# Keeping all seven output-weight phases as split halves in DRAM

## The chip, the cores and the metric

The kernel runs on one core of a Trainium2 chip. The metric is the time of one execution on the device, in microseconds (us); the median of several runs is compared. TensorE (PE) does the matrix products, VectorE (DVE), ScalarE (ACT) and GpSimd (POOL) the rest, and SyncE (SP) issues the transfers between DRAM and on-chip memory.

## What is computed

Two layers on a sequence of 2048 rows of 1024 features in float32: first a gated MLP with mixing in groups of 128 rows, then attention with 16 heads of 64 over bands of nine chunks of 64 rows, with keys and values from the stream between the two, and a final norm. The change lies in the last step of the attention layer, the product with `w_out`:

```
q, z = jnp.split(h @ w_qz, 2, axis=-1)
...
o = lax.map(one_chunk, (jnp.arange(n_chunks), q))     # scores + bias, softmax, times v
o = jnp.moveaxis(o, 0, 1).reshape(bsz, s, B_WIDTH)
return (o * jax.nn.silu(z)) @ w_out                   # 2048 x 1024 times 1024 x 1024
...
x = x + chunk_attention_mixer(...)
return rms_norm(x, final_norm_g)
```

## The kernel before

A float32 product is done as three TensorE passes on pairs of reduced-precision numbers: each operand is split into a high part (a cast on ScalarE, `split_in` L228) and a low part (operand minus high part, a subtraction on VectorE, L229), and `mm3` (L111 to L113) adds high times high, high times low and low times high.

The attention stage works on four tiles of 512 rows, t = 0 to 3, and in each on eight head pairs p. For a pair the kernel projects the next pair's q, k and gate (`pj`, weights `raw_b` split to `wh_b` and `wl_b`), makes scores (`s`, L1469), softmax (`pr`, `nm`, `sl`), transposes (`tp`, L1504), copies to `pt` on ScalarE and VectorE (L1508, L1509) and multiplies with V (`pv`, L1529).

The output projection `bo` of a tile uses Strassen's scheme for a 2 by 2 block product: seven phases instead of eight block products, done in the order 1, 7, 2, 6, 5, 4, 3. Each phase has one weight block, loaded in two pieces q = 0, 1 of 512 KB, and two output column blocks jp = 0, 1 of twelve matmuls each. Phases 1, 2 and 3 use plain quarters of `w_out` (`o_raw`): whenever one is used, its raw piece is loaded (`raw_bo`) and split. Phases 4 to 7 use sums of quarters. These are made and split once, early, and their high and low parts are kept in the DRAM tensors `ows`, so that each use loads two pieces of 512 KB and splits nothing.

The projection of tile t (names `bo` with the tile's number; the function is `o_right`) runs in portions between the pairs of tile t+1: that of the third tile, t = 2, runs beside the last tile's attention. For the last tile `last_right` gets the weights (`whbo`, `wlbo`, and `wbo` for phases 5 and 3) and `last_all` does the products, the first of them beside the last pair's softmax. Split weights live in eight rotating slots of tag `T` (`w_tile`), which the projections' `wh_b` and `wl_b` share; a slot takes a new tile when the last reader of the old one is done. In the last tile, phase 2 uses slots of tag `raw`, phase 5 a slot of `V`, phase 3 one of `PT`.

The order of instructions on each engine comes from a scheduler that works on the program before it runs; `on_beat` ties an instruction to the pace of the pair loop. Every transfer is issued by SP, in order, and at most eight are in flight: one waits for the eighth before it.

Of the kernel before, what the change touches and what calls it, by code (L numbers as in the profile page):

```python
# [9 lines left out]
F32 = mybir.dt.float32  # L10
# [12 lines left out]
NT = S // T  # L23
# [10 lines left out]
def trunk_kernel(  # L34
# [19 lines left out]
    nc = tc.nc  # L54
# [10 lines left out]
    }  # L65
    ows = {
        (ph, q): dram.tile([P, 2, 1024], F32, name=f"ows{ph}_{q}")
        for ph in range(4, 8) for q in range(2)
    }
    khd = [  # L70
        [dram.tile([2, P, T], F32, name=f"khd{t}_{p}") for p in range(NPAIR)]
# [49 lines left out]
    sub, add = ALU.subtract, ALU.add  # L121
    tv, tg = nc.vector.tensor_tensor, nc.gpsimd.tensor_tensor
# [70 lines left out]
    def on_beat(ins):  # L193
        if beat:
            tc.add_manual_dep(
                ins.ins, beat[-1],
                mybir.DependencyInfo(mybir.DependencyClass.NoSync, mybir.DependencyReason.DATA),
                reason="order",
            )
        return ins  # L200
# [16 lines left out]
    def w_tile(name):  # L217
        return sh.tile([P, 1024], F32R, tag="T", name=name, bufs=8)
# [3 lines left out]
    def raw_w(t, name):  # L222
        if t:
            return raws[0].tile([P, 1024], F32, tag="wr", name=name, bufs=2)
        return sh.tile([P, 1024], F32, tag="raw", name=name, bufs=4)

    def split_in(raw, wh, wl):
        hi = nc.scalar.copy(wh[:], raw[:])  # L228
        tv(wl[:], raw[:], wh[:].bitcast(F32), op=sub)  # L229
        return hi  # L230
# [26 lines left out]
    o_raw = {1: (0, 0), 2: (1, 0), 3: (1, 1)}  # L257

    def o_right(t):
        def right(ph):  # L260
            if (t, ph) in o_early:
                return o_early.pop((t, ph))
            out = []
            for q in range(2):
                name = f"bo{t}_{ph}_{q}"
                w = [w_tile(f"w{i}_{name}") for i in "hl"]
                if ph in o_raw:
                    raw = raw_w(1, f"raw_{name}")
                    nc.sync.dma_start(raw[:], wb_out[o_raw[ph]][q])
                    hi = split_in(raw, *w)  # L270
                    if (ph, q) == (1, 1):
                        on_beat(hi)
                else:
                    for i in range(2):
                        nc.sync.dma_start(w[i][:].bitcast(F32), ows[ph, q][:, i, :])
                out.append(w)
            return out
        return right
# [105 lines left out]
    with ExitStack() as actx:  # L384
# [21 lines left out]
        sub, add, mul = ALU.subtract, ALU.add, ALU.mult  # L406
# [650 lines left out]
        tv, tg = nc.vector.tensor_tensor, nc.gpsimd.tensor_tensor  # L1057
# [303 lines left out]
    with ExitStack() as bctx:  # L1361
# [16 lines left out]
        def half_tile(tag, name, bufs, dtype=F32):  # L1378
            return sb.tile([P, 512], dtype, tag=tag, name=name, bufs=bufs)
# [157 lines left out]
        def drain_all():  # L1537
            while drains:
                drains.pop(0)()
# [28 lines left out]
        def square_all(every=False):  # L1568
            if every:
                squares.extend(young)  # L1570
                young.clear()
            while squares:
                on_beat(squares.pop(0)())
            squares.extend(young)
            young.clear()

        owed_out = []

        def send(dst, src):
            if la:  # L1580
                owed_out.append((dst, src))
            else:
                nc.sync.dma_start(dst, src)

        def send_all():
            while owed_out:
                on_beat(nc.sync.dma_start(*owed_out.pop(0)))
# [96 lines left out]
        def last_right(ph, q):  # L1684
            name = f"bo_{ph}_{q}"
            if ph == 5:
                v = sb.tile([P, 8, 256], F32R, tag="V", name=f"w{name}", bufs=2)
                w = [v[:, i * 4 : i * 4 + 4, :].rearrange("p a b -> p (a b)") for i in range(2)]
            elif ph == 3:
                if q == 0:  # L1690
                    lw["pt"] = sb.tile([P, 5376], F32R, tag="PT", name=f"w{name}", bufs=1)
                w = [lw["pt"][:, (2 * q + i) * 1024 : (2 * q + i + 1) * 1024] for i in range(2)]
            elif ph == 2:
                w = [
                    sh.tile([P, 1024], F32R, tag="raw", name=f"w{i}{name}", bufs=4)[:]
                    for i in "hl"
                ]
            else:
                w = [w_tile(f"w{i}{name}")[:] for i in "hl"]
            if ph in o_raw:  # L1700
                raw = raw_w(NT - 1, f"raw_{name}")
                nc.sync.dma_start(raw[:], wb_out[o_raw[ph]][q])
                nc.scalar.copy(w[0], raw[:])
                tv(w[1], raw[:], w[0].bitcast(F32), op=sub)
            else:
                for i in range(2):
                    nc.sync.dma_start(w[i].bitcast(F32), ows[ph, q][:, i, :])
            lw[ph, q] = w

        lviews = {}  # L1710
# [13 lines left out]
        def last_all():  # L1724
# [6 lines left out]
            for q in range(2):  # L1731
                last_right(7, q)
# [164 lines left out]
        def take(gen, n):  # L1897
            for _ in range(n):
                if next(gen, gen) is gen:
                    return  # L1900

        def run(gen):
            for _ in gen:
                pass
# [16 lines left out]
        def ahead(t, p):  # L1921

            if t > 1 and p == 0:
                next(outs[t - 1])
            if p + 1 < NPAIR:
                yield from project(t, p + 1)
                values(t, p + 1)
                for q in GATES[t][p]:
                    yield from gate(t, q)
                if (t, p) == (1, 4):  # L1930
                    next(outs[0])
                yield from some(outs[t - 1], SHARE[t][p])
            elif t + 1 < NT:
                yield from some(outs[t - 1], SHARE[t][p])
                yield from border(t)
                yield from project(t + 1, 0)
                values(t + 1, 0)
                yield from gate(t + 1, 0)
            else:
                yield from some(outs[t - 1], SHARE[t][p] - 6)  # L1940
                last_first()
                yield from some(outs[t - 1], 6)
                yield from some(outs[t], 13)

        def steps_of(t, p):
            n = 24
            if p + 1 < NPAIR:
                n = 16 + 8 * len(GATES[t][p])
            elif t + 1 == NT:
                n = 13  # L1950
            return n + SHARE[t][p]
# [11 lines left out]
        for t in range(NT):  # L1963
            for p in range(NPAIR):
                gen = ahead(t, p) if t + p else first
                total = steps_of(t, p) - (0 if t + p else 8)
                per = 11 if p + 1 == NPAIR and t + 1 < NT else 16
                todo = []
                if t + 1 == NT and p + 1 == NPAIR:
                    o_early[t - 1, 3] = o_right(t - 1)(3)  # L1970
                    todo = last_open()
                if t == 1 and p < 4:
                    todo = o_sums(p, lambda n: half_tile("C", n, 4), lambda n: half_tile(
                        "S", n, 4, F32R
                    ))
                if (t, p) == (0, 3):
                    nc.sync.dma_start(gf[:], fin_g.partition_broadcast(P))
                done = 0
                for u in range(8):
                    if u < 6:  # L1980
                        score(t, p, u + 2)
                    elif p + 1 < NPAIR or t + 1 < NT:
                        score(t + (p + 1) // NPAIR, (p + 1) % NPAIR, u - 6)
                    upto = total * (2 * u + 1) // per
                    take(gen, upto - done)
                    done = max(done, upto)
                    if u == 4:
                        value(t, p, 0)
                    elif u == 0 and before:
                        value(*before, 1)  # L1990
                    flip(t, p, u)
                    drain_all()
                    send_all()
                    square_all()
                    if u and finals:
                        finals.pop(0)()
                    if todo:
                        todo.pop(0)()
                    upto = total * (2 * u + 2) // per
                    take(gen, upto - done)  # L2000
                    done = max(done, upto)
                if t + 1 < NT or p + 1 < NPAIR:
                    run(gen)
                before = t, p
# [61 lines left out]
```

## Time and profile before

| | |
|---|---|
| median of three runs | 2646.81 us (2646.17 to 2648.61) |
| the profiled execution | 2649.25 us, of which the span of work is 2647.5 |
| granted TensorE clock | 0.997 of full speed |
| TensorE busy | 2607.3 us, 98% of the span |
| VectorE, ScalarE, GpSimd busy | 71%, 49%, 34% |
| moved by DMA | 718.74 MB, on average 271 GB/s |

The profile is of one execution. Times in it count from the start of the span. A group row has line, engine, operation, output and inputs by the program's names, count, then busy us and the mean ns of one, then the engine's idle time before these instructions and what ended it. A row of waits has the waiting engine and line, the releaser, and the waiting time in us, the number of waits and the longest. Rows of DMAs end with the median us from issue to landing. Attention on the last tile takes the stretch from about 2300 to 2605 us; from there only the last projection and the final norm are left.

### The profile page before, as it was taken

Reading aid. Unit: us, or ns where it says so; the run is one execution under the profiler, and the core shown is the slowest. Engines: PE = TensorE matmul, PEld = TensorE weight load, DVE = VectorE, ACT = ScalarE, POOL = GpSimd, SP = SyncE. Lnnn points to the kernel's source line nnn. Section 1 sums busy time; section 2 is a strip of 40 time slices with the busy share of each in tenths; the row PEclk is TensorE's granted clock in tenths of the full one; section 3 lists DMA queues with packets and bytes.
Section 4 is the critical chain, followed back from the end, with each engine's and each line's share of the span. In section 5 each row is a group of like instructions: output and inputs, shape, how many; then the busy total and the mean of one; then the engine's idle time right before and its main releaser. Section 6 shows DMA issues by size and latency. Waiting matters only on the chain. (4 is left out here: it accounts for less than half of the span.)

```text
span 2647.5 us, 38028 instructions
## 1 busy us (share of the span) xinstructions
PE 2607.3 (98%) x12976; PEld 2179.8 (82%) x12976; DVE 1889.1 (71%) x2946; ACT 1303.1 (49%) x2303; POOL 893.7 (34%) x874
## 2 busy tenths in 40 slices
PE   8999999999999999999999999999999999999997
PEld 7888888888888888888878778888888888888886
DVE  6655676766767668757777767778778777877677
ACT  5422243443433434343356456666666655666564
POOL 4611335143152322203234434344332232332245
PEclk9999999999999999999999999999999999999999
DMA  7898998989988868967776587778787666875666
GB/s 291 313 347 331 345 367 321 315 324 340 335 318 294 311 235 328 328 201 270 282 266 209 194 284 229 233 240 264 251 269 258 224 208 220 256 229 159 195 227 249
DMA packets 273857, 718.74 MB, mean 271 GB/s; under 512 B 28800, under 2 KB 68736, under 8 KB 273664
## 3 DMA queue, kind: packets, MB, share of 16 engines
q1 hardware_dynamic: 273664, 716.31, 78.2%
q8 instruction: 104, 1.70, 0.3%
q14 instruction: 89, 0.73, 0.1%
HBM read 531.12 MB, written 174.59 MB: 267 GB/s over the span
## 5 line engine op out<-in xcount | busy, mean ns | idle before, releaser
L111 PE MATMUL P<-T,S 128*128 128x512 f32 x1248 | 495.7, 397 | 0.0
L113 PE MATMUL P<-T,S 128*128 128x512 f32 x1248 | 488.1, 391 | 0.1
L112 PE MATMUL P<-T,S 128*128 128x512 f32 x1248 | 487.8, 391 | 0.2 <-DVE T L444 0.2
L1488 POOL TENSOR_SCALAR pr<-pr,sl 128x640 f32<-128x640 f32 (+4 forms) x256 | 206.9, 808 | 553.9 <-DVE sl L1487 467.4
L111 PE MATMUL pj<-hh_b,wh_b 128*128 128x512 f32 x768 | 319.9, 417 | 0.7 <-ACT wh_b L228 0.7
L113 PE MATMUL pj<-hh_b,wl_b 128*128 128x512 f32 x768 | 304.2, 396 | 0.8 <-DVE wl_b L229 0.7
L112 PE MATMUL pj<-hl_b,wh_b 128*128 128x512 f32 x768 | 302.9, 394 | 0.1
L1484 ACT ACTIVATE pr<-pr,nm 128x640 f32<-128x640 f32 (+4 forms) x256 | 195.5, 764 | 186.2 <-DVE nm L1477 184.8
L113 PEld LDWEIGHTS P<-T,S 128*128 128x128 f32 x1248 | 234.6, 188 | 50.9 <-DVE S L444 0.4
L112 PEld LDWEIGHTS P<-T,S 128*128 128x128 f32 x1248 | 235.3, 189 | 45.3 <-DVE T L444 0.6
L111 PEld LDWEIGHTS P<-T,S 128*128 128x128 f32 x1248 | 235.2, 188 | 44.8 <-DVE x L577 0.4
L1509 DVE TENSOR_TENSOR pt<-tp,pt 128x640 fp32r<-128x640 f32 (+4 forms) x256 | 188.5, 736 | 43.8 <-ACT pt L1508 41.2
L1477 DVE CUSTOM_DVE_ANT_0 pr<-s,bias 128x640 f32<-128x640 f32 (+4 forms) x256 | 188.1, 735 | 32.5 <-PE s L1469 27.2
L1508 ACT CAST pt<-tp 128x640 fp32r<-128x640 f32 (+4 forms) x256 | 159.0, 621 | 54.1 <-PE tp L1504 49.7
L1504 PE MATMUL tp<-ident,pr 128*128 128x128 f32 x1120 | 166.5, 274 | 9.6 <-DVE pt L1509 7.8
L113 PEld LDWEIGHTS pj<-hh_b,wl_b 128*128 128x128 f32 x768 | 144.4, 188 | 35.7 <-DVE wl_b L229 2.9
L1504 PEld LDWEIGHTS tp<-ident,pr 128*128 128x128 f32 x1120 | 130.6, 140 | 44.3 <-issue 14.6
L111 PEld LDWEIGHTS pj<-hh_b,wh_b 128*128 128x128 f32 x768 | 145.3, 189 | 18.8 <-ACT wh_b L228 2.4
L1529 PEld LDWEIGHTS pv<-pt,V 128*128 128x128 f32 x896 | 143.0, 188 | 20.2 <-DVE pt L1509 3.2
L112 PEld LDWEIGHTS pj<-hl_b,wh_b 128*128 128x128 f32 x768 | 145.3, 189 | 16.9 <-DVE hl_b L186 0.5
L1529 PE MATMUL pv<-pt,V 128*128 128x256 f32 (+3 forms) x896 | 153.9, 319 | 1.9 <-ACT pt L1508 1.0
L229 DVE TENSOR_TENSOR wl_b<-raw_b,wh_b 128x1024 fp32r<-128x1024 f32 x96 | 120.2, 1253 | 28.2 <-ACT wh_b L228 27.0
(302 smaller groups left out, 5732.7 us busy)
## 6 DMA issues: line engine op xcount, KB each, us to landing
S<-hsd SPq DMA_DIRECT2D x288, 512.0 KB, 5.5
rw<-in_w_a SPq DMA_DIRECT2D x108, 512.0 KB, 6.5
A<-ytd SPq DMA_DIRECT2D x72, 512.0 KB, 5.8
raw_b<-wk SPq DMA_DIRECT2D x72, 512.0 KB, 4.3
hsd<-S SPq DMA_DIRECT2D x56, 512.0 KB, 4.7
V<-vhd SPq DMA_DIRECT2D x56, 512.0 KB, 5.6
bias<-reld SPq DMA_DIRECT2D x64, 320.0 KB, 3.9
va<-vd SPq DMA_DIRECT2D x32, 512.0 KB, 6.0
```

Source lines behind the costliest of these rows:

```text
L111: first = mm(ps, lh, rh, start=first, stop=False)
L112: mm(ps, lh, rl, start=False, stop=False)
L113: mm(ps, ll, rh, start=False, stop=last)
L229: tv(wl[:], raw[:], wh[:].bitcast(F32), op=sub)
L1477: nc.vector.tensor_tensor_reduce(out=pr[:, c0:].rearrange("p (a b) -> p a b", a=nseg), in0=ps[:, :nseg, :w], in1=bias[:, c0:].rearrange("p ...
L1484: nc.scalar.activation(pr[:, c0:], pr[:, c0:], AF.Exp, scale=-1.0, bias=nm[:], accum_out=sl[:])
L1488: nc.gpsimd.tensor_scalar(pr[:, c0:], pr[:, c0:], sl[:], 1.0, op0=ALU.mult, op1=ALU.mult)
L1504: ins = tpose(tp[:, b, :], pr[:, b * P : (b + 1) * P], ident[:])
L1508: nc.scalar.copy(oh, tp[:, b0:5, :].rearrange("p a b -> p (a b)"))
L1509: nc.vector.tensor_tensor(pt[:, 2560 + o + b0 * P : 2560 + o + 640], tp[:, b0:5, :].rearrange("p a b -> p (a b)"), oh.bitcast(F32), op=ALU ...
L1529: mm(po[:, q0 * P : q1 * P], vtl[t, p][:, i, hs], rhs, start=(i == blocks[0] and j == 0), stop=(i == 7 and j == 1),)
```

## The change

`ows` gets entries for phases 1 to 3. The splits are kept where they are made: those of phase 3 in the second tile's projection, those of phases 1 and 2 in the third tile's. Each gives four stores of 512 KB (two pieces, high and low), twelve in all, queued in `halves_out` and issued from ScalarE, one per step of the pair loop. The third tile's phase 3 and the last tile's phases 1, 2 and 3 load halves and split nothing: eight casts and eight subtractions are gone, and eight raw loads are sixteen loads of halves.

```diff
     ows = {
         (ph, q): dram.tile([P, 2, 1024], F32, name=f"ows{ph}_{q}")
-        for ph in range(4, 8) for q in range(2)
+        for ph in range(1, 8) for q in range(2)
     }
...
                 w = [w_tile(f"w{i}_{name}") for i in "hl"]
-                if ph in o_raw:
+                if ph in o_raw and (t, ph) != (2, 3):
                     raw = raw_w(1, f"raw_{name}")
                     nc.sync.dma_start(raw[:], wb_out[o_raw[ph]][q])
                     hi = split_in(raw, *w)
                     if (ph, q) == (1, 1):
                         on_beat(hi)
+                    if (t, ph) in ((2, 1), (2, 2), (1, 3)):
+                        halves_out.extend(
+                            (ows[ph, q][:, i, :], w[i][:].bitcast(F32)) for i in range(2)
+                        )
                 else:
                     for i in range(2):
                         nc.sync.dma_start(w[i][:].bitcast(F32), ows[ph, q][:, i, :])
...
         owed_out = []
+        halves_out = []
...
                 w = [w_tile(f"w{i}{name}")[:] for i in "hl"]
-            if ph in o_raw:
-                raw = raw_w(NT - 1, f"raw_{name}")
-                nc.sync.dma_start(raw[:], wb_out[o_raw[ph]][q])
-                nc.scalar.copy(w[0], raw[:])
-                tv(w[1], raw[:], w[0].bitcast(F32), op=sub)
-            else:
-                for i in range(2):
-                    nc.sync.dma_start(w[i].bitcast(F32), ows[ph, q][:, i, :])
+            for i in range(2):
+                nc.sync.dma_start(w[i].bitcast(F32), ows[ph, q][:, i, :])
             lw[ph, q] = w
...
                     send_all()
+                    if halves_out:
+                        on_beat(nc.scalar.dma_start(*halves_out.pop(0)))
                     square_all()
```

The scheduler's order changes around these places. Names in the rows that follow have lost the tile's number; `wh_bo_1_0` is the high part of phase 1, piece 0. The line numbers after the change are 4 to 5 higher.

ScalarE beside the third tile's phase 1, in the last tile's second pair. Before:

```order
L228 CAST wh_bo_1_1_22775<-raw_bo_1_1_22777 128x1024
L1508 CAST pt_1_22661<-tp_1_3_22816 128x640
L1484 ACTIVATE pr_2_1_22801,sl_2_1_22803<-pr_2_1_22801,nm_2_1_22802 128x640
L1847 COPY ou_1_0_22814<-bo_1_0_22781 128x512
L337 CAST Sho_7_0_22839<-A_s_22450 128x512
L1484 ACTIVATE pr_2_2_22848,sl_2_2_22850<-pr_2_2_22848,nm_2_2_22849 128x640
L228 CAST wh_b_2_1_22856<-raw_b_2_1_22855 128x1024
L1484 ACTIVATE pr_2_3_22909,sl_2_3_22911<-pr_2_3_22909,nm_2_3_22910 128x640
```

After, the same stretch:

```order
L228 CAST wh_bo_1_1_22785<-raw_bo_1_1_22787 128x1024
L1994 DMA ows_0_102<-wh_bo_1_0_22779 128x1024
L1512 CAST pt_1_22671<-tp_1_3_22826 128x640
L1488 ACTIVATE pr_2_1_22811,sl_2_1_22813<-pr_2_1_22811,nm_2_1_22812 128x640
L1846 COPY ou_1_0_22824<-bo_1_0_22791 128x512
L341 CAST Sho_7_0_22850<-A_s_22460 128x512
L1488 ACTIVATE pr_2_2_22859,sl_2_2_22861<-pr_2_2_22859,nm_2_2_22860 128x640
L228 CAST wh_b_2_1_22867<-raw_b_2_1_22866 128x1024
L1994 DMA ows_0_102<-wl_bo_1_0_22780 128x1024
L1488 ACTIVATE pr_2_3_22921,sl_2_3_22923<-pr_2_3_22921,nm_2_3_22922 128x640
```

Two stores have come in; the cast `wh_b_2_1` writes the slot that the first of them reads, and the subtraction `wl_b_2_1` on VectorE the slot of the second.

TensorE at the same place, from the first use of `wh_b_2_1`. Before:

```order
L111 MATMUL pj_2_1_22861<-hh_b,wh_b_2_1_22856 128x512
L112 MATMUL pj_2_1_22861<-hl_b,wh_b_2_1_22856 128x512
L1529 MATMUL pv_1_22865<-pt_1_22661,V_0_22347 128x512 x4
L113 MATMUL pj_2_1_22861<-hh_b,wl_b_2_1_22857 128x512
L1529 MATMUL pv_1_22865<-pt_1_22661,V_0_22347 128x128 x2
```

After:

```order
L111 MATMUL pj_2_1_22872<-hh_b,wh_b_2_1_22867 128x512
L112 MATMUL pj_2_1_22872<-hl_b,wh_b_2_1_22867 128x512
L1533 MATMUL pv_1_22876<-pt_1_22671,V_0_22357 128x512 x4
L1533 MATMUL pv_1_22876<-pt_1_22671,V_0_22357 128x128 x2
L1533 MATMUL pv_1_22876<-pt_1_22671,V_0_22357 128x256 x2
L1533 MATMUL pv_1_22876<-pt_1_22671,V_0_22357 128x384 x4
L1533 MATMUL pv_1_22876<-pt_1_22671,V_0_22357 128x256 x2
L1533 MATMUL pv_1_22876<-pt_1_22671,V_0_22357 128x128 x2
L1473 MATMUL s_3_0_22949<-K_1_1_22694,Ql_1_1_22570 128x320 x2
L113 MATMUL pj_2_1_22872<-hh_b,wl_b_2_1_22868 128x512
```

The first use of `wl_b_2_1` (L113) has moved behind twelve `pv` and two score matmuls.

SP before the last tile's first phases. Before:

```order
L1633 DMA A_hh<-ogd_145 128x512 x2
L1583 DMA x2d_1_155<-ou_7_0_23202 128x512
L1702 DMA raw_bo_0_25247<-in_wb_out 128x1024
L1702 DMA raw_bo_1_25253<-in_wb_out 128x1024
L1821 DMA y_1_25218<-x2d_1_155 128x1024
L1707 DMA wbo_0_25456<-ows_0_104 128x1024
L1587 DMA x2d_3_157<-ou_7_1_23567 128x512
L1707 DMA wbo_0_25456<-ows_0_104 128x1024
L1702 DMA raw_bo_0_25358<-in_wb_out 128x1024
```

After:

```order
L1638 DMA A_hh<-ogd_151 128x512 x2
L1592 DMA x2d_3_163<-ou_7_1_23581 128x512
L1820 DMA y_1_25232<-x2d_1_161 128x1024
L1706 DMA whbo_0_25259<-ows_0_102 128x1024
L1706 DMA wlbo_0_25260<-ows_0_102 128x1024
L1706 DMA whbo_1_25263<-ows_1_103 128x1024
L1706 DMA wlbo_1_25264<-ows_1_103 128x1024
L1592 DMA out<-y_1_25232 128x512 x2
```

Phase 1's two raw loads have become four loads of halves, and they stand behind the store `x2d_3` and the load `y_1`. The very end of TensorE's queue is mixed anew too: before, the last phase's column block `bo_0` is done before `bo_1` starts; now the two alternate, and `bo_0` ends five matmuls before `bo_1`.

## The prediction

> **What bounds the kernel now.** I read the page's busy times first.
>
> ```profile
> span 2647.5 us, 38028 instructions
> PE 2607.3 (98%) x12976; PEld 2179.8 (82%) x12976; DVE 1889.1 (71%) x2946; ACT 1303.1 (49%) x2303; POOL 893.7 (34%) x874
> ```
>
> TensorE idles 40 us in all, so the change can win only where TensorE waits. Next I read windows over the two kinds of place that it touches: the last tile's early head pairs, beside which the third tile's phase 1 runs and stores are put in, and the end, where splits go. After the window and its length stand the busy times of PE, PEld, DVE, ACT and POOL, then clock, DMA share and GB/s.
>
> ```profile
> 2345.00:2375.00 30.00, 29.87 (x162) 25.18 (x161) 22.61 (x42) 19.35 (x34) 10.39 (x12) 1.00 0.81 265
> 2560.00:2605.00 45.00, 38.94 (x208) 31.18 (x207) 41.53 (x70) 29.97 (x56) 25.11 (x24) 1.00 0.87 293
> 2580.00:2590.00 10.00, 8.36 (x43) 6.62 (x44) 10.00 (x18) 6.56 (x13) 4.53 (x5) 1.00 0.81 280
> 2590.00:2600.00 10.00, 8.08 (x50) 6.70 (x48) 9.84 (x16) 5.93 (x12) 7.23 (x7) 1.00 0.96 324
> 2600.00:2610.00 10.00, 9.27 (x50) 7.51 (x48) 5.99 (x14) 4.52 (x8) 1.86 (x3) 1.00 0.96 326
> 2610.00:2620.00 10.00, 10.00 (x46) 8.29 (x45) 7.74 (x12) 3.37 (x9) 6.12 (x6) 1.00 1.01 389
> 2620.00:2630.00 10.00, 10.00 (x46) 8.29 (x45) 6.28 (x10) 4.78 (x11) 9.69 (x7) 1.00 0.42 156
> ```
>
> In the first of them TensorE is full (29.87 of 30) and VectorE and ScalarE have room. In the 45 us from 2560, the last head pair's softmax runs beside the first phases of the last projection: TensorE idles 6.06 there, VectorE is busy 41.53, and from 2580 to 2600 it is the bound (10.00 and 9.84 of 10). From 2610 to 2630 TensorE is full again. The waits of TensorE from 2560 on, and the costliest groups of the work that the change removes, name what it waits for.
>
> ```profile
> PE tp L1504 <- DVE pt L1509: 3.6, 5, 1.1
> PE bo L112 <- DVE wbo L1704: 1.3, 2, 0.7
> PE s L1469 <- DVE nm L1477: 1.1, 2, 0.7
> L1704 DVE TENSOR_TENSOR wlbo<-raw_bo,whbo 128x1024 fp32r<-128x1024 f32 x4 | 5.7, 1433 | 0.0
> L229 DVE TENSOR_TENSOR wl_bo<-raw_bo,wh_bo 128x1024 fp32r<-128x1024 f32 x2 | 4.0, 1991 | 0.0
> L1704 DVE TENSOR_TENSOR wbo<-raw_bo,wbo 128x1024 fp32r<-128x1024 f32 x2 | 3.9, 2010 | 0.0
> L1703 ACT CAST whbo<-raw_bo 128x1024 fp32r<-128x1024 f32 x4 | 4.2, 1047 | 2.7 <-DMA raw_bo<-in_wb_out 1.8 <-PE bo L113 0.9
> ```
>
> TensorE waits for `pt` and `nm`, softmax work that shares VectorE with these splits, and 1.3 us for the last weights' own split.
>
> **The change, part by part.** *Splits before 2605.* Two subtractions of the third tile's phase 3 (4.0) and four of the last tile's phases 1 and 2 (5.7) go: 9.7 us of VectorE's 41.53, with six casts of about 1.05 from ScalarE, which has 15 us free there. The gain is at most the 6.06 that TensorE idles. It is nothing if each wait is the latency of one transpose, copy and multiply and not queueing; the rows for that hop are these.
>
> ```profile
> L1508 ACT CAST pt<-tp 128x640 fp32r<-128x640 f32 x10 | 6.9, 689 | 2.6 <-PE tp L1504 2.5
> L1509 DVE TENSOR_TENSOR pt<-tp,pt 128x640 fp32r<-128x640 f32 x10 | 8.1, 812 | 0.5 <-ACT pt L1508 0.4
> ```
>
> One hop is 0.69 + 0.81 = 1.5 us, with idle time of 0.4 before the multiply, so the multiply mostly stood behind other VectorE work. With 31.8 of 45 left, queueing lessens but doesn't vanish, and the hop stays. I take half: -3.0 (ends -6.06 and 0).
>
> *Phase 1's loads.* Before, two raw loads went out ahead of `x2d<-ou` and `y<-x2d`. Now four loads of 512 KB stand behind both on SP, and wait for slots of tag T.
>
> ```profile
> 2569.33 1.51 SPq L1702 DMA_DIRECT2D raw_bo<-in_wb_out  x2
> 2571.63 0.33 SPq L1821 DMA_DIRECT2D y<-x2d  x1
> 2577.68 0.32 SPq L1587 DMA_DIRECT2D x2d<-ou  x1
> 2585.42 0.39 PE L111 MATMUL bo<-whbo,Qho 128*128 128x512 f32 x1
> DMA to landing us min/median/max: 4.8/7.6/9.7
> ```
>
> The last row is that of `whbo`. `x2d<-ou` waits for a VectorE result that stood behind the 4.0 us of phase 3's splits, so I expect it near 2575 and the loads from there on; 4.8 to 7.6 later is 2580 to 2583, the fourth some 2 later, with their first use at 2583 to 2585.4. The ends are 0 and +4 (2577.7 + 9.7 = 2587.4 against 2583); I take +0.7, since the middle lands about in time. Phases 7 and 6 stand behind them with the same DMA work, and I add nothing.
>
> *Phase 3's loads.* The 1.3 us of waiting for its split goes. Instead of two raw loads there are four of halves, at the end of a stretch in which the DMA share is 0.96 to 1.01.
>
> ```profile
> 2612.68 1.61 SPq L1702 DMA_DIRECT2D raw_bo<-in_wb_out  x2
> 2631.01 0.39 PE L111 MATMUL bo<-wbo,Qho 128*128 128x512 f32 x1
> DMA to landing us min/median/max: 3.5/6.3/11.3
> ```
>
> The last row is that of `raw_bo`; the second raw load, issued by 2614, had landed by 2614 + 11.3 = 2625.3. One more MB at 389 GB/s is 2.7 us, so 2628, against a use at 2631.0 less the 3 won above. This just holds: -1.3, ends -1.3 and +2. A gain above 3 would begin to be eaten here.
>
> *The end.* The order now mixes the two last column blocks: the first ends five matmuls before the second, not twelve, so its eviction and norm no longer lie under matmuls.
>
> ```profile
> 2637.08 0.68 DVE L1877 TENSOR_TENSOR row<-bo,ou 128x512 f32<-128x512 f32 x1
> 2640.82 1.42 DVE L1827 SCALAR_TENSOR_TENSOR row<-row,rr_f,gf 128x512 f32<-128x512 f32 x2
> 2643.16 1.42 DVE L1827 SCALAR_TENSOR_TENSOR row<-row,rr_f,gf 128x512 f32<-128x512 f32 x2 [0.66 <-POOL rr_f L126]
> ```
>
> The first block's eviction (0.68) started at 2637.08, now about seven matmuls (1.6 us) later against the end; VectorE has gaps of 0.66 there, which take up part. I take +0.7, ends 0 and +1.6.
>
> *Twelve stores.* ScalarE issues no DMA before; SP's issues bound the price of one.
>
> ```profile
> L1707 SPq DMA_DIRECT2D wlbo<-ows x6: 382/405/442, 2588.0 to 2611.5; - x6
> L228 ACT CAST wh_bo<-raw_bo x1: 1061/1061/1061, 2347.6 to 2347.6; 128x1024 fp32r<-128x1024 f32 x1
> 2354.46 1.03 ACT L228 CAST wh_b<-raw_b 128x1024 fp32r<-128x1024 f32 x1
> 2355.53 1.23 DVE L229 TENSOR_TENSOR wl_b<-raw_b,wh_b 128x1024 fp32r<-128x1024 f32 x1
> 2357.27 0.39 PE L113 MATMUL pj<-hh_b,wl_b 128*128 128x512 f32 x1
> 2357.50 1.75 PE L1529 MATMUL pv<-pt,V 128*128 128x128 f32 x12
> 2363.81 0.46 PE L1469 MATMUL s<-K,Ql 128*128 128x320 f32 x2
> hsd<-S SPq DMA_DIRECT2D x56, 512.0 KB, 4.7
> vhd<-v SPq DMA_DIRECT2D x32, 512.0 KB, 3.5
> ```
>
> At 0.33 (`y<-x2d`, above) to 0.44 each, twelve are 4 to 5.3 us, a third of them in each of three places; ScalarE is busy 19.35 of 30 in the first window, so this costs TensorE 0 (ends 0 and +1). What matters is that a slot of tag T now takes its next weights only when its store has landed. Beside the third tile's phase 1 (the last tile's second pair) the next writers come at once: the store of `wl_bo_1_0` is queued behind the cast of `wh_b_2_1`, at 2355.5, and the subtraction `wl_b_2_1`, which ran at 2355.53, writes that slot. Stores of 512 KB landed in 3.5 us (`vhd<-v`) and 4.7 (`hsd<-S`). With 4.7 the subtraction runs from 2360.2 to 2361.4. The order gives TensorE the twelve `pv` and two score matmuls first, 1.75 + 0.46, so it needs the result at 2357.27 + 2.2 = 2359.5 and waits 1.9; with 3.5, 0.7. Behind that subtraction on VectorE stand `pt`, `og` and the next `pr`, and `wl_b_2_0` after `Ql_2_0`, for which I add 0.6. Taken: +2.5, with ends 0.7 and 12 (second rival). In the two other places at least two softmax blocks stand between store and next writer: 0, ends -0.5 and +1.
>
> The Trainium skill, page "DMA: Bandwidth & Descriptors", section "Issuing engines are not separate DMA queues", says that DMAs started by ScalarE and SP share the same 16 engines, so that a second issuer saves only its sequencer's time. By it the stores compete with the loads of a window that already has a share of 0.81; the sum would have the slower landing of the second rival.
>
> *Sum.* -3.0 + 0.7 - 1.3 + 0.7 + 0 + 2.5 + 0 = -0.4 us. The profiled execution took 2649.25 with a span of 2647.5, so 2648.85 for its like; the median of the runs, 2646.81, lies 2.44 lower, and the prediction is 2646.4.
>
> **The rivals.** *VectorE's relief is worth all of it (faster).* All 6.06 and 1.27 us go, loads are in time and stores cost nothing: 2646.81 - 7.3 = 2639.5. For it: VectorE at 10.00 of 10 just where TensorE loses most. Against: the 1.5 us hop, the loads at a share near 1, and the slot that waits for a store. Chance 0.16 for over 5.3 us.
>
> *The stores hold slots for long (slower).* Place: beside the third tile's phase 1. Each us of landing beyond 2.8 keeps TensorE waiting a us, as worked out above: 2355.5 + landing + 1.23 - 2359.5. Loads among many others took up to 9.7 and 11.3. The first store, issued when the cast of `wh_bo_1_1` ends (2347.6 + 1.06 = 2348.7), makes the cast of `wh_b_2_1`, due at 2354.46, late from a landing of 5.8, and with it ScalarE's queue and the second store. At 10 that is 7.2 + 4.2 + 0.6 = 12, or +9.5 over my sum: 2656. It decides from a landing of 8: 5.2 + 2.2 + 0.6 = 8 gives 2652, 5.3 over before. For it: the share of 0.81. Against: the medians 3.5 and 4.7. Chance 0.16. In the same Trainium skill page, section "Anatomy of one DMA — SWDGE (gpsimd) path", the completion of a write to DRAM is said to wait for the write's receipt and to be surprisingly long at times; by it the landing would be the later. The rows of `hsd<-S` (4.7) and the loads around it don't show such a delay.
>
> *The splits' time turns into waits for loads (about no change).* The last phases wait for transfers instead of for VectorE: -3.0 becomes -1, -1.3 becomes 0, and the rest stays: 2646.81 - 1 + 0.7 + 0.7 + 2.5 = 2649.7. For it: shares of 0.96 to 1.01 from 2590 to 2620. Chance 0.2. That the change doesn't do what it says is excluded: the order has eight casts and eight subtractions less, and twelve stores more.
>
> **The numbers.** My own case, terms near the values taken, has 0.48; its range is 2643 to 2650. Within 0.2% (5.3 us, about what a measurement tells from no change) lie this and the third rival: 0.68. Faster: 0.16; slower: 0.16. From 2641 to 2652.5 little more than a tenth is left out at each end.
>
> **What would show it.** Right: VectorE below 33 of 45 in the window from 2560 and TensorE's idle time there near 3; no wait for L1704; no wait of `bo` over 1 us at its first phase; a wait of 1 to 3 us of `pj` L113 for `wl_b` L229 in the last tile's second pair, with a landing of `ows<-wl_bo` of 4 to 5 us. Wrong: a landing over 8, waits of TensorE at phase 1, 7 or 3 for a DMA, or idle time after 2560 that stays at 6.

## The result, and the profile after

| | before | after |
|---|---|---|
| median of the runs, us | 2647.72 (2645.21 to 2651.55, 22 runs) | 2652.47 (2647.34 to 2656.86, 22 runs) |
| ratio to before | | 1.0015, interval 1.0009 to 1.0021 |
| profiled execution, us | 2649.25 | 2653.25 |

By the ratio the change made the kernel slower by 4.0 us (2.4 to 5.6 by the interval); the medians lie 4.75 us apart, since the ratio is not their quotient. That is less than the 0.2% that the prediction took as the limit of a measurement, but 22 runs of each resolve it. The forecast was no change, 2646.4, with a range of 2643 to 2650 for its own case, and 2652.47 lies above that range.

The first lines of the page after:

```profile
span 2651.5 us, 38027 instructions
PE 2607.3 (98%) x12976; PEld 2179.4 (82%) x12976; DVE 1873.7 (71%) x2938; ACT 1296.2 (49%) x2295; POOL 893.9 (34%) x874
```

TensorE's busy time is the same to the tenth; VectorE lost 15.4 us of work and ScalarE 6.9. So the change took away what it said, and TensorE now waits more in other places. Windows show where. Columns: window, length, busy PE, PEld, DVE, ACT, POOL, granted clock, DMA share, GB/s. First before, in two places that the prediction had not shown, then after:

```profile
2345.00:2400.00 55.00, 54.85 (x302) 46.52 (x301) 39.15 (x73) 33.93 (x59) 17.02 (x22) 1.00 0.61 200
2605.00:2648.00 43.00, 32.21 (x144) 25.90 (x143) 29.58 (x49) 13.80 (x30) 21.75 (x18) 0.92 0.58 220
```

```profile
2345.00:2400.00 55.00, 51.42 (x271) 42.98 (x271) 35.26 (x65) 31.21 (x54) 17.06 (x19) 0.97 0.67 222
2560.00:2605.00 45.00, 41.78 (x226) 34.58 (x225) 34.44 (x69) 24.80 (x51) 23.95 (x26) 1.00 0.93 317
2605.00:2652.00 47.00, 34.29 (x151) 26.27 (x148) 32.19 (x45) 13.28 (x30) 20.20 (x17) 0.91 0.77 295
```

From 2560 to 2605 TensorE idles 3.22 us instead of 6.06: the relief is there. From 2345 to 2400, beside the third tile's phase 1, it idles 3.58 instead of 0.15, and the granted clock is 0.97 on average. TensorE's waits after name the cause, first from 2345 to 2400, then from 2560 on (total us, number, longest):

```profile
PE pj L113 <- DVE wl_b L229: 3.2, 2, 2.3
PE pj L111 <- ACT wh_b L228: 0.3, 1, 0.3
```

```profile
PE bo L112 <- DMA wlbo<-ows: 1.6, 1, 1.6
PE s L1473 <- DVE nm L1481: 1.6, 1, 1.6
PE bo L113 <- DVE Qlo L346: 0.3, 1, 0.3
```

TensorE waits for the subtraction `wl_b`; the waits for `pt` and for the last weights' split (`wbo`, 1.3) are gone, and a wait of 1.6 for phase 7's halves has come. The timeline after, row by row (start, duration, what; in brackets the idle time before it and what ended it), shows what `wl_b` waits for:

```profile
2352.18 0.33 ACTq L1994 DMA_DIRECT2D ows<-wl_bo  x1
2352.88 1.04 ACT L228 CAST wh_b<-raw_b 128x1024 fp32r<-128x1024 f32 x1
2358.81 1.22 DVE L229 TENSOR_TENSOR wl_b<-raw_b,wh_b 128x1024 fp32r<-128x1024 f32 x1 [3.82 <-DMA ows<-wl_bo]
2360.09 0.76 PE L113 MATMUL pj<-hh_b,wl_b 128*128 128x512 f32 x1 [2.32 <-DVE wl_b L229]
2360.66 0.63 PE L111 MATMUL pj<-hh_b,wh_b 128*128 128x512 f32 x1
2363.85 0.39 PE L113 MATMUL pj<-hh_b,wl_b 128*128 128x512 f32 x1
2371.15 0.50 PE L113 MATMUL pj<-hh_b,wl_b 128*128 128x512 f32 x1 [0.86 <-DVE wl_b L229]
```

The cast is done by 2353.92, but the subtraction stands until 2358.81, when the store that reads its slot has landed, and VectorE idles 3.82 us in front of it. TensorE waits 2.32 us. Behind that wait a matmul lasts 0.63 instead of 0.39.

To compare kernels I cut the last 360 us of each profiled execution at the starts of named matmuls: A from the third tile's first projection (`pj` of its first pair) to the last tile's first, where phase 3's halves are stored; B from there to the projection of the last tile's sixth pair, where those of phases 1 and 2 are stored; C from there to the end of the last matmul, where the splits are gone; D from the last matmul to the end of the span. Each row below is one execution. What lies earlier scatters by more than the change is worth, though the change adds and removes nothing there: A starts at 1996.2 us in e3 and at 2002.6 us in e7.

| us | A | B | C | D |
|---|---|---|---|---|
| before | 290.34 | 167.94 | 180.13 | 8.98 |
| after | 291.70 | 173.48 | 177.13 | 11.56 |
| e1 stores only | 292.48 | 173.53 | 179.48 | 9.25 |
| e2 no stores | 290.23 | 168.68 | 176.94 | 11.27 |
| e3 TensorE's end tied | 292.07 | 171.79 | 177.80 | 11.85 |
| e4 bigger `ows` | 290.73 | 169.08 | 179.44 | 9.02 |
| e5 VectorE's end tied | 292.28 | 173.93 | 174.79 | 10.53 |
| e6 two stores per step | 295.14 | 171.28 | 175.26 | 11.55 |
| e7 phase 3 only | 293.09 | 167.64 | 176.34 | 9.30 |
| e8 all halves early | 290.59 | 167.70 | 175.25 | 10.27 |
| e9 one store less | 290.82 | 170.85 | 175.56 | 11.55 |
| e10 no stores, end tied | 289.71 | 169.33 | 177.13 | 10.25 |
| e11 phases 2 and 3, end tied | 289.84 | 168.26 | 175.31 | 9.74 |
| e12 phase 3 early, end tied | 290.79 | 168.41 | 177.34 | 9.62 |

The granted clock is a part of these lengths, besides TensorE's waits: in some executions it falls to 0.50 for 3.41 us, which costs up to 1.7 us (half of that time). Such a dip lies in B of after, e1 and e5, in A of e6 (from 1998.8 us, long before that kernel's first store at 2267.6), and in C of e3, e7, e10 and e12. The one of e6:

```profile
1998.90:2002.00 3.10, 3.10 (x9) 2.52 (x9) 3.10 (x4) 3.10 (x5) 1.27 (x1) 0.50 0.91 296
```

### The profile page after: what moved, and what is told of

Same layout as the page of the kernel before. It is cut to its first block, busy times and chain, and to the rows that moved or that the text cites. A ratio compares the mean times of both kernels' runs of the same rounds, so it can differ in the third digit from the quotient of the medians.

```text
span 2651.5 us, 38027 instructions
## 1 busy us (share of the span) xinstructions
PE 2607.3 (98%) x12976; PEld 2179.4 (82%) x12976; DVE 1873.7 (71%) x2938; ACT 1296.2 (49%) x2295; POOL 893.9 (34%) x874
## 5 line engine op out<-in xcount | busy, mean ns | idle before, releaser
L113 PE MATMUL P<-T,S 128*128 128x512 f32 x1248 | 488.2, 391 | 0.1
L113 PE MATMUL pj<-hh_b,wl_b 128*128 128x512 f32 x768 | 304.9, 397 | 4.5 <-DVE wl_b L229 4.4
L113 PEld LDWEIGHTS P<-T,S 128*128 128x128 f32 x1248 | 234.6, 188 | 51.0 <-DVE S L448 0.4
L113 PEld LDWEIGHTS pj<-hh_b,wl_b 128*128 128x128 f32 x768 | 144.5, 188 | 40.0 <-DVE wl_b L229 7.6
```

What stands on the lines that cost most here:

```text
L113: mm(ps, ll, rh, start=False, stop=last)
```

## The experiments

Each edit is against the changed kernel, where nothing else is said. Medians are set beside those of the kernel before on the same chip; the ratio is the one on record, and where it differs from the quotient of the medians, it and its interval count. Differences from the changed kernel are differences of two such ratios.

**e1: the stores alone.** The last tile loads raw pieces and splits them as before, and so does the third tile's phase 3; the twelve stores stay.

```diff
-                if ph in o_raw and (t, ph) != (2, 3):
+                if ph in o_raw:
...
+            if ph in o_raw:
+                raw = raw_w(NT - 1, f"raw_{name}")
+                nc.sync.dma_start(raw[:], wb_out[o_raw[ph]][q])
+                nc.scalar.copy(w[0], raw[:])
+                tv(w[1], raw[:], w[0].bitcast(F32), op=sub)
+            else:
                 for i in range(2):
                     nc.sync.dma_start(w[i].bitcast(F32), ows[ph, q][:, i, :])
```

> The twelve stores are made, but the third tile's phase 3 and the last tile load raw quarters and split them as before. Theory A (slots held by stores cost the time beside the third tile's phase 1): 3.4 us over before, TensorE idle 3.4 us from 2345 to 2400 and 6 us from 2560 to 2605 as before. Rival B (the added loads near the end and their transfers cost it): at most 1 us over before.

Measured: 2651.72 against 2647.90, ratio 1.0015 (1.0006 to 1.0023). The stores cost what the whole change costs. The wait is the same, to the hundredth of a us:

```profile
PE pj L113 <- DVE wl_b L229: 3.1, 2, 2.3
```

C and D are those of before (179.48, 9.25), A and B those of after.

**e2: the loads without the stores.** The third tile's phase 3 and the last tile's phases 1 to 3 load the halves of phases 4 to 6 instead, which need no store.

```diff
-                    if (t, ph) in ((2, 1), (2, 2), (1, 3)):
-                        halves_out.extend(...)
...
-                nc.sync.dma_start(w[i].bitcast(F32), ows[ph, q][:, i, :])
+                nc.sync.dma_start(w[i].bitcast(F32), ows[ph if ph > 3 else ph + 3, q][:, i, :])
```

> No stores; the third tile's phase 3 and the last tile's phases 1 to 3 load the halves of other phases, so the loads and the end are those of the change, with other data (the output is not the reference's). Theory A: 3.4 us under the changed kernel, that is 0.5 to 1 us over before; idle under 0.5 us beside the third tile's phase 1, and from the last matmul to the end 11.7 us as in the changed kernel. Rival B: stays about 4 us over before.

Measured: 2645.62 against 2647.90, ratio 0.9993 (0.9984 to 1.0001), so 1.9 us under before and not the 0.5 to 1 us over it that were expected. Between after and e2 lie about 6 us, and from 2345 to 2400 one wait is left:

```profile
PE tp L1504 <- DVE pt L1509: 0.2, 1, 0.2
```

e1 and e2 together settle the cause: the stores, not the loads. Their sizes, +4.0 and -1.9 us, add up to the +4.0 of the change only within the intervals.

**e3: TensorE's end in the old order.** From phase 6 on, each column block of the last tile is tied behind the one before.

```diff
+                        if i >= 6 and k == 0:
+                            tc.add_manual_dep(ins.ins, prev[0].ins.name, ...)
```

> The changed kernel, with the last tile's column blocks from phase 6 on tied to follow each other as they did before the change. Theory A (the mixed order of the last blocks lengthens the chain behind the last matmul from 9.0 to 11.7 us): 2 to 2.7 us under the changed kernel, 9 us from the last matmul to the end. Rival B (late loads set the end): no gain, since TensorE then waits for the weights by as much more.

Measured: 2652.31 against 2647.90, ratio 1.0018 (1.0009 to 1.0027). The gain of 2 to 2.7 us that was expected did not come. D is 11.85, no shorter, though the two column blocks no longer mix. So TensorE's order at the end, to which the prediction gave its +0.7, is not the cause. The timeline of VectorE from TensorE's last matmul on shows another:

```profile
2637.47 0.39 PE L115 MATMUL bo<-wbo,Qlo 128*128 128x512 f32 x1
...
2638.72 0.68 DVE L1885 TENSOR_TENSOR row<-bo,ou 128x512 f32<-128x512 f32 x1
...
2641.26 1.41 DVE L1835 SCALAR_TENSOR_TENSOR row<-row,rr_f,gf 128x512 f32<-128x512 f32 x2 [0.66 <-POOL rr_f L128]
2642.59 0.68 DVE L1885 TENSOR_TENSOR row<-bo,ou 128x512 f32<-128x512 f32 x1
...
2645.13 1.41 DVE L1835 SCALAR_TENSOR_TENSOR row<-row,rr_f,gf 128x512 f32<-128x512 f32 x2 [0.66 <-POOL rr_f L128]
```

The last eviction (L1885) runs 4.7 us after the last matmul ended, since in VectorE's order it stands behind another row block's norm, which waits for a chain over ScalarE and GpSimd.

**e4: only the larger `ows`.** The program of before, with the added entries unused.

```diff
-        for ph in range(4, 8) for q in range(2)
+        for ph in range(1, 8) for q in range(2)
```

(This diff is against before.)

> The kernel before with six more entries in ows that nothing uses, so that only places in DRAM can move. Theory A: within 0.5 us of before. Rival C (the 1.2 us that TensorE idles more before 1900 us come from other places in DRAM): 1.2 us over before, with 1.2 us more idle time before 1900.

Measured: 2648.58 against 2647.90, ratio 0.9999 (0.9990 to 1.0008). No effect of where things lie in DRAM is seen; the interval leaves room for about 2.6 us either way, but B and D stay near those of before.

**e5: VectorE's end tied.** The norm of row block 3 goes behind the eviction of the last column block.

```diff
-                    if last:
+                    if last and b == 3:
+                        pass
+                    elif last:
...
-                    tv(o, ps, y, op=add)
+                    got = tv(o, ps, y, op=add)
+                    if last and (ph, jp) == (3, 1):
+                        finish(3, got.ins.name)
```

> The changed kernel with one edit: in the last tile the norm of row block 3 is tied behind the eviction of the very last column block on VectorE's queue. Theory A (the 2.6 us behind the last matmul come from VectorE's queue, in which the norms stand ahead of the last evictions, not from TensorE's order): 9 us or less from the last matmul to the end instead of 11.6, and 2 to 2.9 us under the changed kernel. Rival B (that chain is set by the work of two row blocks that now end together): 11 us or more stay, no gain.

Measured: 2648.75 against 2647.30, ratio 1.0001 (0.9992 to 1.0010). The end of before, of after, then of e5:

```profile
2638.10 0.39 PE L113 MATMUL bo<-wbo,Qlo 128*128 128x512 f32 x1
2640.07 0.68 DVE L1877 TENSOR_TENSOR row<-bo,ou 128x512 f32<-128x512 f32 x1
```

```profile
2639.52 0.39 PE L113 MATMUL bo<-wbo,Qlo 128*128 128x512 f32 x1
...
2640.68 1.41 DVE L1826 SCALAR_TENSOR_TENSOR row<-row,rr_f,gf 128x512 f32<-128x512 f32 x2 [0.66 <-POOL rr_f L126]
2642.01 1.28 DVE L1876 TENSOR_TENSOR row<-bo,ou 128x512 f32<-128x512 f32 x2
```

```profile
2637.36 0.39 PE L113 MATMUL bo<-wbo,Qlo 128*128 128x512 f32 x1
2637.49 1.28 DVE L1884 TENSOR_TENSOR row<-bo,ou 128x512 f32<-128x512 f32 x2
2640.03 2.74 DVE L1828 SCALAR_TENSOR_TENSOR row<-row,rr_f,gf 128x512 f32<-128x512 f32 x4 [0.59 <-POOL rr_f L126]
```

The last two evictions now start with the last matmul (2637.49) instead of 2.1 us after its end (before, the last one starts 1.6 us after it), but the norms that were ahead of them now come after, and D falls only from 11.56 to 10.53, not to the 9 expected. The order on VectorE is a part of the longer end; 1.5 us of it stay, and their cause is open. The rest of the gain is in C (174.79, 2.3 less than after): TensorE idles 2.0 us less there, with waits of 1.0 for `nm` and 0.5 for phase 7's halves where after has 1.6 each. Why these waits are shorter is not explained.

**e6: two stores per step.** The stores leave sooner after the split.

```diff
-                    if halves_out:
+                    for _ in range(min(2, len(halves_out))):
```

> The changed kernel with two stores per step of the pair loop instead of one, so that a piece's low half is stored with its high half. Theory A (the slot that the low half holds is what the next split waits for): idle time from 2345 to 2400 falls from 3.6 to under 1 us, 2.5 to 4 us under the changed kernel. Rival B (any twelve stores cost this much by their transfers): no more than 1 us under the changed kernel.

Measured: 2652.08 against 2647.30, ratio 1.0016 (1.0007 to 1.0025). In B the wait for `wl_b` is one of 1.4 instead of two that sum to 3.2, and B is 2.2 shorter (171.28); most of that is the clock, which does not dip in this B. A is 3.4 longer (295.14): half of it is the dip at 1998.8, which no store can have caused, and half is that TensorE idles 1.7 us more. The gain of 2.5 to 4 us that was expected is not there. From 2240 to 2345 the waits sum to 3.5, where after has one of 0.9, beside the stores of phase 3's halves:

```profile
PE tp L1508 <- DVE pt L1513: 2.6, 2, 1.8
PE bo L113 <- DVE Slo L346: 0.9, 1, 0.9
```

What delays `pt` there I did not find.

**e7: phase 3's halves alone.** Only the second tile's phase 3 is stored; the last tile splits phases 1 and 2 as before.

```diff
-                    if (t, ph) in ((2, 1), (2, 2), (1, 3)):
+                    if (t, ph) in ((1, 3),):
...
+            if ph in (1, 2):
+                raw = raw_w(NT - 1, f"raw_{name}")
...
```

> Only phase 3 is kept as halves: four stores in the second tile's projection, loads in the third's and the last tile's; phases 1 and 2 are split at each use as before. Theory A: no wait beside the third tile's phase 1 (-5 us against the changed kernel there), 1 to 1.5 us for its four stores, about 1.5 us of the gain after 2560 left, the wait for the last split gone (-1.2), the longer chain behind the last matmul (+2.6): 0 to 2 us over before. Rival B (the loads of phases 1 and 2 are what costs, not the stores): 2 us or more under before.

Measured: 2645.83 against 2647.30, ratio 0.9993 (0.9985 to 1.0002). B is that of before (167.64). The time is 1.9 us under before (4.0 under to 0.5 over), between the two expectations. The longer end that was expected (+2.6) did not come: D is 9.30, without any tie. So phase 3's loads alone don't lengthen the end.

**e8: all halves made beside the second tile's first pairs**, with e5's tie. No store stands beside the last tile.

```diff
-                if ph in o_raw and (t, ph) != (2, 3):
...
+                if True:
...
-            combine(b11, b12, b11), combine(b12, b22, b12), combine(b22, b22, b11),
+            kept_first(1, b11, combine(b11, b12, b11)),
+            kept_first(3, b22, combine(b12, b22, b12)),
+            kept_first(2, b21, combine(b22, b22, b11)),
```

> All seven phases' halves are made once, where those of phases 4 to 7 are made (beside the second tile's first four pairs, stored from their own buffers by SP); no tile splits a quarter of w_out after that, no store holds a slot of tag T, and the end has the edit of the run with the tied norm. Theory A: the stores' 5 us go, the gain after 2560 (3 us) and of the end (2.6 us) stay: 3 to 6 us under before. Rival B (24 more splits of 512 columns and 12 MB more of loads in the second tile cost as much there): within 1 us of before.

Measured: 2648.67 against 2647.30, ratio 1.0001 (0.9993 to 1.0010). This is rival B's case. A and B are those of before, but the second tile's stretch (from its first `pj` to the third tile's) takes 289.58 instead of about 284.7, the mean of the kernels that leave it alone: making and storing the halves costs 4.9 us there. The cost is moved, not removed.

**e9: one store less.** The low half of phase 1's first piece, the store seen in the timeline above, is not made; the last tile loads another phase's low half in its place.

```diff
+                            if (t, ph, q, i) != (2, 1, 0, 1)
...
+                nc.sync.dma_start(w[i].bitcast(F32), ows[4 if (ph, q, i) == (1, 0, 1) else ph, q][:, i, :])
```

> The changed kernel without one of its twelve stores, that of the low half of phase 1's piece 0 (the last tile loads another phase's low half in its place, so the output is not the reference's). Theory A (this one store holds the slot that the next split waits for; TensorE's wait for it, 2.3 us, is also long enough to halve its granted clock for 3.4 us): the wait of pj for wl_b near 2360 goes, the clock stays at 1.00 there, and the stretch from the last tile's start to its sixth pair takes 168 to 169 us instead of 173; 3.5 to 5 us under the changed kernel. Rival B (the other stores of the place take over the wait): under 1.5 us of gain.

Measured: 2648.25 against 2647.48, ratio 1.0008 (0.9999 to 1.0016). That is 1.9 us under the changed kernel, between the two expectations. B is 170.85, 2.6 less than after but not the 168 to 169 expected, and in the 15 us from 2360 the clock is 1.00. The window, then TensorE's waits from 2345 to 2400:

```profile
2360.00:2375.00 15.00, 13.60 (x72) 11.35 (x73) 11.02 (x21) 7.86 (x15) 6.62 (x5) 1.00 0.94 264
```

```profile
PE tp L1509 <- DVE pt L1514: 1.4, 1, 1.4
PE pj L113 <- DVE wl_b L229: 0.9, 1, 0.9
```

This one store of twelve carries about half of B's cost in these two executions, 1.1 us of it by TensorE's idle time and most of the rest by the clock; two shorter waits, for the next slot and for `pt`, carry the other half.

**e10: e2 with e5's tie.** Both edits together:

```diff
-                nc.sync.dma_start(w[i].bitcast(F32), ows[ph, q][:, i, :])
+                nc.sync.dma_start(w[i].bitcast(F32), ows[ph if ph > 3 else ph + 3, q][:, i, :])
...
+                    if last and (ph, jp) == (3, 1):
+                        finish(3, got.ins.name)
```

> No stores (the third and the last tile load the halves of other phases, so the output is not the reference's) and VectorE's last norm tied behind the last eviction. Theory A: what the loads and the missing splits are worth by themselves, without the stores and the longer end: 4 to 6 us under before, of it 3 us or more from the last tile's sixth pair to the end. Rival B (the gain of the two edits is one and the same): 2 to 3 us under before, as without the end's edit.

Measured: 2644.21 against 2647.48, ratio 0.9990 (0.9981 to 0.9999): 2.6 us faster, less than the 4 to 6 expected if both costs went entirely, and as much as rival B named. D is still 1.3 above that of before.

**e11: phases 2 and 3 as halves, phase 1 split as before, with e5's tie.**

```diff
-                    if (t, ph) in ((2, 1), (2, 2), (1, 3)):
+                    if (t, ph) in ((2, 2), (1, 3)):
...
+            if ph == 1:
+                raw = raw_w(NT - 1, f"raw_{name}")
+                ...
```

> Phases 2 and 3 are kept as halves, phase 1 is split at each use as before, and VectorE's last norm is tied behind the last eviction. Theory A: no wait beside the third tile's phase 1, 2 us for phase 3's stores, nothing for phase 2's, 3 us gained after the last tile's sixth pair: 0.5 to 2 us under before. Rival B (the loads of phase 2 land too late): level with before or over it.

Measured: 2644.80 against 2647.48, ratio 0.9992 (0.9983 to 1.0001). B is 168.26 though phase 2's four stores lie in it: B's cost is that of phase 1's stores alone, whose slots the next pair's weights take at once. With e7 this is the fastest of the versions that load their own halves, 2.1 us under before as e7 is 1.9 under, and neither is clearly apart from before.

**e12: phase 3's halves made beside the second tile's first pairs, phases 1 and 2 split as before, with e5's tie.**

```diff
-            combine(b11, b12, b11), combine(b12, b22, b12), combine(b22, b22, b11),
+            combine(b11, b12, b11),
+            kept_first(3, b22, combine(b12, b22, b12)),
+            combine(b22, b22, b11),
...
```

(This diff is against before.)

> Phase 3's halves are made once, beside the second tile's first four pairs, and no tile splits phase 3; phases 1 and 2 are split at each use; the end has the same edit. Theory A: about 1.3 us lost in the second tile (a third of the 4 us that all three phases cost there), no stores from slots of tag T, 3 us gained at the end: 1.5 to 3 us under before. Rival B (the second tile's added work costs as much as it saves): within 1 us of before.

Measured: 2646.22 against 2647.48, ratio 1.0001 (0.9992 to 1.0009). The 1.5 to 3 us expected did not come; it is rival B's case. The second tile's stretch is 287.62, 3 us longer, about what C gains (2.8).

## Why the prediction was wrong

The sum was -0.4 and the measured change is +4.0. The mechanism of the loss was forecast, and its place; what failed are two costs in the sum. The term of the twelve stores was taken as +2.5 and measured +4.8 beside the third tile's phase 1, mostly since it had no term for the clock, with likely 1.4 more beside phase 3, which was taken as nothing. The term of the end was taken as +0.7 and measured +2.5, and its reason (TensorE's order) was wrong. By stretches, from the means over the kernels that share a property, one execution each (e6 and e9, whose stores of phase 1 differ, are left out of B, and e6 of A):

| stretch | predicted | measured | from |
|---|---|---|---|
| B: stores of phases 1 and 2 | +2.5 | +4.8 | 173.18 (after, e1, e3, e5) against 168.38 (the eight kernels without phase 1's stores) |
| A: stores of phase 3 | 0 | +1.4 | 291.75 (after, e1, e3, e5, e7, e9, e11) against 290.40 (before, e2, e4, e8, e10, e12) |
| C: splits gone, halves loaded | -3.6 | -3.3 | 176.37 (after, e2, e3, e5, e6, e9, e10) against 179.68 (before, e1, e4) |
| D: the end | +0.7 | +2.5 | 11.56 (after, e2, e3, e6, e9) against 9.08 (before, e1, e4) |
| sum | -0.4 | +5.4 | inside the 2.4 to 5.6 that the runs give |

*The stores beside the third tile's phase 1: right place, mis-sized.* The chain was as forecast: store, subtraction `wl_b`, `pj` L113, a wait of 1 to 3 us. It measured 2.32 (forecast 1.9), and the second and third waits 0.86 and 0.26 (forecast 0.6 together), 3.4 in sum. Two errors cancelled on the way. I had the store start behind the cast, at 2355.5; it was issued at 2352.18, before the cast in front of it in ScalarE's order started (2352.88). And it took 6.5 us, where I took 4.7:

```profile
L1994 ACTq DMA_DIRECT2D ows<-wl_bo x6: 326/326/363, 2269.3 to 2440.0; - x6
...
DMA to landing us min/median/max: 2.6/3.6/6.5
```

The last row is that of all twelve stores. Their median is what the rows of other stores promised; the one store on which the sum hung took the longest. I had priced it by medians of stores taken all over the program, not by transfers in a window with a DMA share of 1.02 (2352 to 2359). The early issue took most of that error back, by luck: in the first wait 0.4 us are left, in the later ones 0.5.

What the sum did not have is the clock, and that is the larger part of the miss. In the windows after, in the idle time before that matmul and from 1 and from 4 us behind it:

```profile
2358.00:2360.00 2.00, 0.00 (x0) 0.00 (x0) 1.19 (x2) 0.79 (x2) 0.00 (x0) 1.00 0.92 280
2361.00:2362.00 1.00, 1.00 (x4) 0.72 (x3) 0.97 (x2) 0.00 (x0) 0.00 (x0) 0.50 1.03 406
2364.00:2365.00 1.00, 1.00 (x8) 0.78 (x7) 0.00 (x0) 0.00 (x0) 0.64 (x1) 1.00 0.96 326
```

For about 3.4 us TensorE ran at a granted clock of 0.50, four matmuls a us instead of eight at the last row's rate: eight matmuls stood 0.43 us apart instead of 0.23, which is 1.6 us. With 3.4 of waits that makes 5.0 of B's 5.5 in this execution. e3 shows B without the dip: the same wait, and in the window a us behind it the full clock (the last section shows what a dip goes with).

```profile
2359.11 0.50 PE L115 MATMUL pj<-hh_b,wl_b 128*128 128x512 f32 x1 [2.34 <-DVE wl_b L231]
2360.00:2361.00 1.00, 1.00 (x6) 0.83 (x5) 0.97 (x2) 0.00 (x0) 0.00 (x0) 1.00 1.00 406
```

There B is 171.79, 1.7 less than in after and e1. I made no kernel that changes the clock alone, so its price rests on these traces. How often a run of the changed kernel has the dip is not known: of the four profiled executions with the same stores there (after, e1, e3, e5) three have it.

*The two other store places: taken as nothing.* A is 1.4 longer in the mean. The groups overlap (289.84 to 293.09 against 289.71 to 290.79), so this term is likely and not shown. e6, where A is worst, is no better evidence, since half of its excess is a dip of the clock before the first store.

*The end: sized too low, and for a wrong reason.* I looked at TensorE's order. e3 put that back and D stayed; e5 moved one norm behind the evictions on VectorE and got back 1.0 of 2.5. What makes the other 1.5 is open; e2 (11.27) and e7 (9.30) together say that it comes with the loads of phases 1 and 2, not with phase 3's.

*Splits and loads: right in the sum, partly by luck.* Idle time from 2560 to 2605 fell by 2.84 us, forecast 3.0, which was half of what TensorE idled there. But I had taken half because the hop of transpose, copy and multiply would stay, and in after no wait for `pt` is left (3.6 before): the relief was worth about 4.4, and a late load took 1.6 of it back. The wait for the last split went. VectorE is busy 34.44 of 45, where I named less than 33. No wait for phase 1's first halves shows in after, but 0.9 to 1.4 in e9, e2 and e6, so the +0.7 for it was a fair middle. Phase 7's halves, which stand behind them and to which I added nothing, came 1.6 late in after and 0.5 in e5; a wait for a DMA at phase 7 was among my signs of being wrong. The C of e3 and e10 in the table's mean holds a dip of the clock each, so C without dips gains somewhat more than 3.3.

*The rivals.* The slower rival had the right mechanism, slots held by stores, but asked for a landing of 8 or more; it took 6.5, plus the clock, plus the end. The measured +4.0 lies between its +5.3 at a landing of 8 and the +2.9 of the third rival (the splits' time turns into waits for loads, 2649.7). The third rival's reason did not hold: most of the relief stayed.

## What to carry to other kernels

A store from a working buffer is a reader of that buffer until it has landed. Before adding one, name the next writer of each slot and price the wait by the slowest transfer in that window, not by the median of the program; stores whose slots are not taken at once (phase 2's, e11) were free. A wait near 2 us can cost more than its length: the clock took another 1.6 here. When work is taken off an engine near the end, look at the order that is left on that engine between the last matmul and the end: that order, not TensorE's, took back part of the gain here.

## What the runs showed of the hardware

- The clock records of the traces hold only 0.50 and 1.00, and each dip between two stretches of 1.00 lasts 3.41 us. All changes within an execution lie on a grid of 3.413 us (before has dips from 50.02 and from 1586.02 us, 450 steps apart). What goes with a dip is TensorE's idle time within one step of that grid, not the length of one wait. In the fourteen profiled executions, from 20 us on up to the last matmuls, each of the 18 steps with 1.8 us of idle time or more was followed by a dip, none with less than 1.4 was, and in between both occur. So dips stand behind waits of 2.32 (after), 2.32 (e1) and 2.81 us (e5), and none behind 2.34 in e3, which the grid cuts into 1.47 and 0.87. Shorter waits sufficed too: 1.82 us in e12, and 1.81 in e10, whose rows are these.

```profile
2584.38 0.56 PE L1469 MATMUL s<-K,Qh 128*128 128x320 f32 x2 [1.81 <-DVE nm L1477]
2585.80:2589.10 3.30, 3.30 (x12) 2.82 (x11) 2.58 (x8) 0.97 (x3) 2.29 (x3) 0.50 0.88 231
```

The Trainium skill, page "TensorE: Matmul & The Clock Gate", section "HAM oscillation — how this bites in real kernels", asks for no idle gap of TensorE above about 3.4 us. The traces do not agree: here gaps of little more than half of that were followed by a clock of 0.50.
- A store issued by ScalarE took 0.33 us of its queue (the median of twelve), and the one at 2352.18 went out 0.7 us before the cast that stands ahead of it in ScalarE's order started.
- Twelve stores of 512 KB landed in 2.6 to 6.5 us in one execution, with a median of 3.6.
